# Layer 0 of a two-layer trunk: half of the gate projection z moved ahead of u, and all embedding units put into one block at the start

## Chip, core and metric

The kernel runs on one core of one Trainium2 chip. The metric is device time in microseconds (us), the median of the runs. Five engines matter: PE (TensorE, matmuls; PEld is its weight load), DVE (VectorE), ACT (ScalarE), POOL (GpSimd) and SP, which here only issues DMAs.

## What is computed

A trunk of two layers over two sequences of 512 tokens, model width 1024. The change lies in layer 0, a Fourier mixer with a gate, and in the embedding product that each layer adds at its end:

```
h = rmsnorm(x, norm_g[0])
u, z = split(h @ w_in)                       # 1024 channels each
f = real(fft2(u over tokens and channels in a group))   # 8 groups of 128
y = einsum('bsgc,gcd->bsgd', f, w_mix)
x = x + (y * silu(z)) @ w_out
x = x + sigmoid(x @ ple_gate_w[0]) * (p[0] @ ple_w[0])
```

Layer 1 (neighbourhood attention with the same kind of gate and embedding) and the final norm follow; the change does not touch them.

## The kernel before

Activations lie channel-major: 8 tiles of 128 channels by 1024 tokens, the two sequences s = 0 and 1 side by side, 512 tokens each. Every fp32 product is made of three passes (`PASSES`, line 29): each operand is split into a high part (a cast on ACT) and a low part (a subtraction on DVE or POOL; `split`, line 109), and high*high, high*low and low*high are accumulated. A product of one 128-channel output unit with one sequence over all 8 input tiles is thus 24 matmuls of 128x512.

**Embedding units.** `ple_units` (line 170) makes 16 units, n = 8*s + u, of 6 matmuls each: p[0] @ ple_w[0] for output tile u and sequence s. A unit is copied out of PSUM by ACT and stored to a DRAM scratch by SP. Before, three units come with the squares of x for the norm, and the others are handed out one at a time between the steps that follow (`next(ples)`).

**Norm.** The squares of x are made on ACT and added on DVE or POOL into accumulators (`sumsq`, line 160). `stats_sums` (line 139) adds them over channels with matmuls that have 2 columns; ACT takes the root, DVE the reciprocal (`stats_rows`), four PE transposes spread the row over partitions (`stats_bcast`) and ACT copies it to `rb`. This is done once for each sequence.

**Preparation of h.** For each item (k, s), tile k of sequence s: `h_scale` on DVE, `h_fold` (sums of token t and 512-t on DVE, differences on POOL, two single columns on POOL), `h_hi` (cast on ACT), `h_lo` (subtraction on DVE or POOL). The 16 items go in the order of `items` (line 257). h is kept folded, as even and odd parts over tokens.

**u.** Its weights are folded over channels in the same way (`w_fold`, line 282) and split (`w_split`, line 292). `u_step(hf, k)` (line 365) multiplies the folded h of tile k with half hf of the u weights: 27 matmuls of 252 or 260 columns into 7 PSUM banks. `first_half` (line 375) holds the order by hand: it interleaves the preparation of h, the folding of weights, the u steps of half 0 and the remaining embedding units. PE and DVE keep program order there (`pins`); ACT, POOL and SP are ordered by the compiler's scheduler. Half 1 follows, 8 more steps.

**Fourier products.** For each of 8 channel groups gi and each s: 12 matmuls into `z`, split, 6 matmuls into `yp`, and ACT copies `yp` to the tile y[gi] (line 481).

**z.** For u = 0 to 7 and each s, 24 matmuls into a PSUM tile `zg`, which uses h still in its folded form (line 497). Then the unfolding: ACT halves the odd part into `zo`, DVE makes three small operations into `zt`, ACT applies silu, DVE multiplies by y[u], and the result is split (cast on ACT, subtraction on POOL) into yz[u] (line 508). PE is not pinned there: the scheduler places z matmuls between Fourier products. The tiles of this stage (pools f2 and f2t) use memory that the Fourier stage holds to its end.

**Output.** For each of 8 output tiles and each s, 24 matmuls `og` over k = 0 to 7 of yz[k] (line 520). The weights of each z or output unit are loaded in two tiles of 256 KB, cast by ACT and split by POOL; four such tiles (`whl`) exist at a time.

Of the kernel before, what the change touches and what calls it, by code (L numbers as in the profile page):

```python
# [10 lines left out]
F32 = mybir.dt.float32  # L11
# [6 lines left out]
P = 128  # L18
# [14 lines left out]
def kernel(ctx: ExitStack, tc: tile.TileContext, xT, pT0, pT1, gains, w_u, w_l0, w_ple0,  # L33
# [35 lines left out]
    BM = ((KD - 1,), (0, KD - 1))  # L69
# [120 lines left out]
    # ------------------------------------------------------------------ layer 0: Fourier mixer  # L190
# [44 lines left out]
    ple_split(0)  # L235
    ples = ple_units(0, ph, plw, f0, ple_psum, PEB)
    for k in range(KD):
        sq = sumsq(accs[0], k, xk[k][:, 0:TOK], TOK, f0, v, hold=(k == 7), nb=SQB)
        if k in (3, 5, 7):
            next(ples)  # L240
    rw = stats_rows(stats_sums([accs[0], sq], TOK, f0, ups, "e10"), TOK, f0)
    next(ples)
    plw.append([])
    for raw in raws:
        hl = f0.tile([P, 2, 512], F32R, name="hl", tag="hlx", bufs=2)
        split(hl, raw, g)
        plw[1].append(hl)
    rbs = []

    def bcast(rw, tag):  # L250
        rb = f0.tile([P, TOK], F32, name="rb", tag="rb", bufs=2)
        a.copy(out=rb, in_=stats_bcast(rw, TOK, ups, tag))
        rbs.append(rb)

    bcast(rw, "e11")

    items = [(0, 0), (1, 0), (2, 0), (0, 1), (1, 1), (3, 0), (2, 1), (4, 0), (3, 1), (5, 0), (4, 1), (6, 0), (5, 1),
             (7, 0), (6, 1), (7, 1)]
# [22 lines left out]

    def w_fold(hf, k):
        raw = load_w(w_u[hf, k // 2, :, (k % 2) * 512:(k % 2 + 1) * 512])
        r4 = raw.rearrange("p (g c) -> p g c", g=4)
        wf = wfs[hf, k] = f1t.tile([P, 512], F32, name="wf", tag="wf", bufs=4)
        we = wf[:, 0:4 * NE].rearrange("p (g c) -> p g c", g=4)
        wo = wf[:, 4 * NE:].rearrange("p (g c) -> p g c", g=4)
        v.tensor_tensor(out=we[:, :, 1:64], in0=r4[:, :, 1:64], in1=r4[:, :, 127:64:-1], op=ALU.add)
        g.tensor_copy(out=we[:, :, 0:NE:64], in_=r4[:, :, 0:NE:64])
        g.tensor_tensor(out=wo, in0=r4[:, :, 1:64], in1=r4[:, :, 127:64:-1], op=ALU.subtract)  # L290
# [21 lines left out]
    accB = f0.tile([P, TOK], F32, name="accB")
    for k in range(KD):
        x = xk[k][:, TOK:TT]
        if k == 1:
            a.activation(out=accB, in_=x, func=AF.Square)
        elif k in (3, 5):
            sumsq(accB, k, x, TOK, f0, g, nb=SQB)
        else:
            sq = sumsq(accs[1], k, x, TOK, f0, v, hold=(k == 7), nb=SQB)  # L320
        for f in S1.get(k, ()):
            f()
    rw = stats_rows(stats_sums([accs[1], accB, sq], TOK, f0, ups, "o1"), TOK, f0)
# [51 lines left out]
    def first_half():  # L375
        kf, ks = iter(range(2, KD)), iter(range(2, KD))
        pins.update("pv")
        for i in range(3, len(items) + 2):
            if i - 1 < len(items) and i > 3:
                h_hi(*items[i - 1])  # L380
            if 5 <= i:
                h_lo(*items[i - 2], {'v': v, 'g': g}[LOE[i - 2]])
            if i < len(items):
                h_scale(*items[i])
                h_fold(*items[i])
            if i == 3:
                w_split(0, 1)
            if i in WFI:
                w_fold(0, next(kf))
            if i in WSI:  # L390
                w_split(0, next(ks))
            for k in range(KD):
                if (k, 0) in items[:max(0, i - 1)] and (k, 1) in items[:max(0, i - 1)] and k not in used and (0, k) in whs:
                    used.add(k)
                    next(ples, None)
                    u_step(0, k)
        for k in range(EW):
            w_fold(1, k)
            w_split(1, k)

    used = set()
    ych = []
    gps = Banks(z=(0, 1), yp=(2, 3), g=(4, 5, 6, 7), w=(4, 5, 6, 7, 0, 1, 2, 3))
    with c1:
        for hf in range(2):
            eps_[:] = [[ups_tile(f"e{s}{t}") for t in range(2)] for s in range(NSEQ)]
            ops_[:] = [ups_tile(f"o{s}") for s in range(NSEQ)]
            nps_[:] = [ups_tile("n")]
            if hf == 0:
                first_half()  # L410
            else:
                for k in range(KD):
                    if k >= EW:
                        w_fold(1, k)
                        w_split(1, k)
                    u_step(1, k)
                    if k == 1:
                        dc = load_tables(cs, sgn)
                    if k in (2, 5):
                        load_mix(k // 3, dc, qp)  # L420
            if hf == 0:
                for _ in ples:
                    pass
# [33 lines left out]
        for gi in range(8):  # L457
            y = xp.tile([P, TT], F32, name=f"y{gi}", tag=f"x{gi}")
# [3 lines left out]
            for s in range(NSEQ):  # L462
# [18 lines left out]
                a.copy(out=y[:, s * TOK:(s + 1) * TOK], in_=yp)  # L481
# [6 lines left out]
    with tc.tile_pool(name="f2", bufs=1) as f2, tc.tile_pool(name="f2t", bufs=2) as f2t:  # L488
        yz = []
        for u in range(8):  # L490
            hl = weights(w_l0[u])
            yzk = f2.tile([P, 2, TT], F32R, name=f"yz{u}")
            yz.append(yzk)
            for s in range(NSEQ):
                o = s * TOK
                ps = gps.tile([P, 512], F32, name="zg", tag="w")
                gemm(ps, hl, lambda k, al: h0[k][:, al, o:o + TOK])
                zo = f2t.tile([P, 256], F32, name="zo", tag="zo", bufs=1)
                a.activation(out=zo[:, 0:255], in_=ps[:, 257:512], func=AF.Copy, scale=0.5)
                z = f2t.tile([P, TOK], F32, name="zt", tag="zt")  # L500
                v.tensor_copy(out=z[:, 0:512:256], in_=ps[:, 0:512:256])
                v.scalar_tensor_tensor(out=z[:, 1:256], in0=ps[:, 1:256], scalar=0.5, in1=zo[:, 0:255],
                                       op0=ALU.mult, op1=ALU.add)
                v.scalar_tensor_tensor(out=z[:, 511:256:-1], in0=ps[:, 1:256], scalar=0.5, in1=zo[:, 0:255],
                                       op0=ALU.mult, op1=ALU.subtract)
                a.activation(out=z, in_=z, func=AF.Silu)
                v.tensor_tensor(out=z, in0=z, in1=ych[u][:, o:o + TOK], op=ALU.mult)
                split(yzk[:, :, o:o + TOK], z, g)
        for u in range(8):
            hl = weights(w_l0[8 + u])  # L510
# [51 lines left out]
    with tc.tile_pool(name="f3", bufs=1) as f3:  # L562
# [26 lines left out]
        block = gates(f3, 0, w_l0[16:24], x1h, emit0)  # L589
# [25 lines left out]
    # ------------------------------------------------------------------ layer 1: neighbourhood attention  # L615
# [18 lines left out]
    with ExitStack() as c2:  # L634
# [125 lines left out]
        # key tile, query blocks, and where in the step's pair of key tiles each query block lies  # L760
# [147 lines left out]
    # ------------------------------------------------------------------ layer 1: output, gate, final norm  # L908
# [211 lines left out]
def _layout(i):  # L1120
# [9 lines left out]
    w_l0 = np.concatenate([_units(w_in[:, 1024:]), _units(i["fn_w_out"][0]), _units(i["ple_gate_w"][0])], axis=0)  # L1130
# [7 lines left out]
    for sc in range(4):  # L1138
# [9 lines left out]
        "xT": c(xT), "pT0": c(pT0), "pT1": c(pT1), "gains": c(gains), "w_u": c(w_u), "w_l0": c(w_l0),  # L1148
# [26 lines left out]
```

## Time and profile before

| | before |
|---|---|
| median of 3 runs | 1128.08 us (1127.16 to 1130.82) |
| span of the profiled execution | 1125.8 us |
| PE busy | 1086.9 us, 97% |
| DVE, ACT, POOL busy | 568.8, 583.9, 629.3 us |
| mean granted clock of PE | 0.986 of full |

The profiled execution's own time is its span, 1125.8 us, plus what lies around it; the median of the runs is 2.3 us more than the span. Busy shares are averages over stages with different limits, so they say little about the first stage, which is the one that is edited. Idle time of an engine that does not bound a stage costs nothing.

### The profile page before, as it was taken

How to read it: one execution, taken by the hardware profiler on the slowest of the kernel's cores; microseconds unless marked ns; L12 is line 12 of the kernel's file. 1: busy time of each engine (PE TensorE's matmuls, PEld its weight loads, DVE VectorE, ACT ScalarE, POOL GpSimd, SP SyncE). 2: the span in 40 equal slices, each digit the busy share in tenths (PEclk: the TensorE clock that was granted, in tenths of full speed). 3: DMA queues.
4: the chain of work that ended last, by engine and by line, in shares of the span. 5: the costliest groups of instructions: out<-in, count | busy, mean ns of one | idle time of the engine just before them, and what ended most of it. 6: DMA issues, size and time to landing. Idle time of an engine off the chain costs nothing.

```text
span 1125.8 us, 17630 instructions
## 1 busy us (share of the span) xinstructions
PE 1086.9 (97%) x6028; PEld 934.5 (83%) x6028; DVE 568.8 (51%) x1253; ACT 583.9 (52%) x1083; POOL 629.3 (56%) x530
## 2 busy tenths in 40 slices
PE   6889999999999999999999999999999999999996
PEld 4779998888888888989888788989888886888886
DVE  5984015221123454277777666777766236114445
ACT  7434226332233474367777667768677734222434
POOL 4884216544534656455757475657566446548643
PEclk9889999999999999999999999999999998999998
DMA  8323002123244447547567565757674055322324
GB/s 318 106 89 109 29 20 75 56 60 109 85 146 144 158 151 224 150 128 198 172 170 214 153 197 163 199 167 209 172 217 123 21 196 197 126 97 78 103 65 150
DMA packets 75689, 156.04 MB, mean 139 GB/s; under 512 B 13328, under 2 KB 16016, under 8 KB 75600
## 3 DMA queue, kind: packets, MB, share of 16 engines
q1 hardware_dynamic: 64480, 128.43, 37.1%
q10 hardware_dynamic: 10960, 25.97, 8.0%
q8 instruction: 47, 0.77, 0.3%
q0 software_dynamic: 160, 0.52, 0.1%
q14 instruction: 42, 0.34, 0.1%
HBM read 107.17 MB, written 22.28 MB: 115 GB/s over the span
## 4 chain that ended last, share of the span: by engine, by line
PE 39%; DMA 6%; DVE 3%; ACT 2%; issue 1%; POOL 1%; SPq 0%; ACTq 0%; DVEq 0%; POOLq 0%
PE qg L82 8%; PE og L82 7%; PE gg L82 7%; PE vg L82 4%; PE ops L82 4%; PE zg L82 4%; PE pps L82 2%; PE sps L82 2%; DMA qst<-qh 2%; DMA qst<-ql 1%; DVE sz L82 1%; PE zs L82 1%; DVE x L82 1%; DMA raw<-in_w_na_dram 1%; DMA raw<-yz_d 1%
## 5 line engine op out<-in xcount | busy, mean ns | idle before, releaser
L82 POOL TENSOR_TENSOR hl<-raw,hl 128x512 fp32r<-128x512 f32 x168 | 223.2, 1332 | 181.8 <-ACT hl L82 163.8
L82 POOL TENSOR_TENSOR ptl<-st,pth 128x512 fp32r<-128x512 f32 x128 | 164.3, 1292 | 101.8 <-ACT pth L82 69.1
L82 PE MATMUL qg<-ha,hl 128*128 128x512 f32 x768 | 215.1, 396 | 0.0
L82 PE MATMUL gg<-ha,hl 128*128 128x512 f32 (+1 forms) x840 | 176.6, 371 | 0.0
L82 PEld LDWEIGHTS gg<-ha,hl 128*128 128x128 f32 x840 | 148.2, 188 | 27.2
L82 PE MATMUL zg<-ha,hl 128*128 128x512 f32 x672 | 164.8, 391 | 0.0
L82 ACT CAST hl<-raw 128x512 fp32r<-128x512 f32 x168 | 103.7, 618 | 112.8 <-PE og L82 34.5
L82 DVE CUSTOM_DVE_ANT_0 sps<-sps,bt 128x256 f32<-128x256 f32 x256 | 110.2, 430 | 72.9 <-PE sps L82 67.6
L82 PEld LDWEIGHTS qg<-ha,hl 128*128 128x128 f32 x768 | 130.3, 190 | 14.0
L82 PEld LDWEIGHTS zg<-ha,hl 128*128 128x128 f32 x672 | 121.6, 188 | 21.5
L82 PE MATMUL vg<-hl,ha 128*128 128x256 f32 x768 | 108.1, 282 | 0.0
L82 PEld LDWEIGHTS vg<-hl,ha 128*128 128x128 f32 x768 | 98.8, 190 | 0.1
L82 ACT ACTIVATE st<-st 128x512 f32<-128x512 f32 x128 | 80.8, 632 | 33.1 <-DVE st L82 32.0
L82 PE MATMUL og<-yzk,hl 128*128 128x512 f32 x384 | 91.1, 399 | 2.3 <-POOL yzk L82 1.2
L82 DVE TENSOR_TENSOR st<-pps,bt 128x512 f32<-128x512 f32 x128 | 87.0, 679 | 6.3 <-PE pps L82 6.2
L82 PEld LDWEIGHTS og<-yzk,hl 128*128 128x128 f32 x384 | 73.5, 193 | 19.7 <-POOL hl L82 1.9
L82 PE MATMUL og<-yz,hl 128*128 128x512 f32 x384 | 87.2, 389 | 0.0
L82 PEld LDWEIGHTS og<-yz,hl 128*128 128x128 f32 x384 | 72.1, 188 | 15.0
L82 ACT CAST pth<-st 128x512 fp32r<-128x512 f32 x128 | 79.5, 621 | 3.7 <-ACT qh L82 0.6
L82 DVE TENSOR_TENSOR sg<-sg,pg 128x512 f32<-128x512 f32 (+1 forms) x35 | 32.7, 934 | 87.1 <-ACT sg L82 87.1
L82 PE MATMUL ops<-ptl,vt 128*65 128x256 f32 x256 | 65.9, 280 | 0.0
L82 PE MATMUL ops<-pth,vt 128*65 128x256 f32 x256 | 65.9, 279 | 0.0
(154 smaller groups left out, 1688.4 us busy)
## 6 DMA issues: line engine op xcount, KB each, us to landing
bt<-in_bias_dram ACTq DMA_DIRECT2D x64, 384.0 KB
raw<-in_w_l_dram SPq DMA_DIRECT2D x80, 256.0 KB
raw<-in_w_na_dram SPq DMA_DIRECT2D x64, 256.0 KB
pp_d<-pe SPq DMA_DIRECT2D x32, 256.0 KB
pg<-pp_d SPq DMA_DIRECT2D x16, 512.0 KB
qst<-qh SPq DMA_DIRECT2D x64, 128.0 KB
kst<-kh SPq DMA_DIRECT2D x64, 128.0 KB
x<-in_xT_dram SPq DMA_DIRECT2D x16, 256.0 KB
```

Of the source, the lines that this page charges most:

```text
L82: ins = getattr(self.eng, op)(*args, **kw)
```

## The change

The embedding units become one block of 16 at the start. The table `beside` says what is issued behind each unit: squares, both norms, and the preparation of the first items of h. Outputs of units are copied in turn by DVE and ACT. The weights of the embedding are now all loaded ahead of x.

Then comes the preparation of the other items of h, and beside it z for u = 0 to 3 instead of u: `z_first(k, s)` makes 12 matmuls (4 units, 3 passes) for item (k, s), into 8 PSUM banks that hold the 4 units and both sequences. `z_out` copies them out (ACT), and `z_act` unfolds them and applies silu, beside the u steps of half 0. Half 0 of u now runs as half 1 does, after all of h is ready.

In the Fourier stage the first four groups are multiplied with silu(z) as they leave PSUM (DVE). In the z stage only u = 4 to 7 are left; each pass of its loop also splits y[u - 4]. The single-column copies in `h_fold` and `w_fold` go from POOL to ACT.

```diff
-    BM = ((KD - 1,), (0, KD - 1))
+    BM = ((0, KD - 1), (0, KD - 1))
-    pins.update(PINS)
-    plw = [weights(w_ple0[0])]
+    pins.update("pv")
+    raws = [load_w(w_ple0[0][:, 512 * i:512 * (i + 1)]) for i in range(2)]
     load_p(0)
+    for i in range(2):
+        raws.append(f0.tile([P, TOK], F32, name="h", tag="h", bufs=4))
+        sp.dma_start(out=raws[-1], in_=w_ple0[1][:, 512 * i:512 * (i + 1)])
     load_x(0)
-    raws = [load_w(w_ple0[1][:, 512 * i:512 * (i + 1)]) for i in range(2)]
+    load_p(1)
     load_x(1)
-    load_p(1)
...
+    def ple_out(n, pp, eng):
+        s, u = n // 8, n % 8
+        pe = f0.tile([P, TOK], F32, name="pe", tag="pe", bufs=PEB)
+        if eng is v:
+            v.tensor_copy(out=pe, in_=pp)
+        else:
+            a.copy(out=pe, in_=pp)
+        sp.dma_start(out=pp_d[0][u][:, s * TOK:(s + 1) * TOK], in_=pe)
...
-        g.tensor_copy(out=f[:, 0:512:256], in_=h[:, 0:512:256])
+        a.copy(out=f[:, 0:512:256], in_=h[:, 0:512:256])
...
+    def z_split(k, eng):
+        hl = whs["z", k] = whl.tile([P, 2, 512], F32R, name="hl", tag="hl")
+        split(hl, load_w(w_zk[k]), eng)
...
+    def z_first(k, s, us=range(4)):
+        o = s * TOK
+        for u in us:
+            if k == 0:
+                zps[u, s] = zbank.tile([P, 512], F32, name="zf", tag=f"z{u}{s}")
+            for n, (wl, al) in enumerate(PASSES):
+                mm(zps[u, s], whs["z", k][:, wl, u * P:(u + 1) * P], h0[k][:, al, o:o + TOK],
+                   start=(k == 0 and n == 0), stop=(k == KD - 1 and n == 2))
...
+    def z_out(u, s):
+        if s == 0:
+            zrs.append(xp.tile([P, TT], F32, name=f"zr{u}", tag=f"x{4 + u}"))
+        a.copy(out=zrs[u][:, s * TOK:(s + 1) * TOK], in_=zps.pop((u, s)))
+
+    def z_act(u, s):
...
+        v.tensor_tensor(out=z[:, 1:256], in0=r[:, 1:256], in1=r[:, 257:512], op=ALU.add)
+        g.tensor_tensor(out=z[:, 511:256:-1], in0=r[:, 1:256], in1=r[:, 257:512], op=ALU.subtract)
+        a.activation(out=z[:, 0:512:256], in_=r[:, 0:512:256], func=AF.Silu)
+        for c in (slice(1, 256), slice(257, 512)):
+            a.activation(out=z[:, c], in_=z[:, c], func=AF.Silu, scale=0.5)
...
+    def stat(s):
+        rws[s] = stats_rows(stats_sums([accs[s], accB, sqs[s]], TOK, f0, st_ps, "s"), TOK, f0)
...
+    beside = {
...
+        5: [L(ple_split, 1)],
+        6: [L(stat, 0), L(lambda: bcast(rws[0])), L(square, 0, 1), L(square, 1, 1)],
+        7: [L(h_scale, 0, 0), L(square, 2, 1)],
...
+        11: [L(h_hi, 1, 0), L(h_fold, 2, 0), L(square, 6, 1), L(square, 7, 1)],
+        12: [L(h_lo, 1, 0, g), L(h_hi, 2, 0)],
+        13: [L(stat, 1), L(z_split, 1, g)],
+        14: [L(lambda: bcast(rws[1])), L(h_lo, 2, 0, v)],
+        15: [L(h_scale, 0, 1), L(h_fold, 0, 1)],
+    }
+    prev = None
+    for n in range(16):
+        pp = ple0(n)
+        for f in beside[n]:
+            f()
+        if prev is not None:
+            ple_out(n - 1, prev, (a, v)[n % 2])
+        prev = pp
+    ple_out(15, prev, a)
...
+    for j, (k, s) in enumerate(steps0 + [(6, 1)]):
+        i = next(at)
+        if i < len(items):
+            if i > 3:
+                h_scale(*items[i])
+                h_fold(*items[i])
+            h_hi(*items[i])
+        if 4 <= i and i - 1 < len(items):
+            h_lo(*items[i - 1], (v, g)[i % 2])
+        if i in (4, 6, 8, 10, 12, 14):
+            z_split(i // 2, (g, v)[i // 2 % 2])
+        if k < 6 or s == 0:
+            z_first(k, s)
...
-            if hf == 0:
-                first_half()
...
+            for k in range(KD):
+                nk = k + EW
+                if nk < KD or hf == 0:
+                    w_fold(hf + nk // KD, nk % KD)
+                    w_split(hf + nk // KD, nk % KD)
+                u_step(hf, k)
+                if not hf:
+                    z_act(k // 2, k % 2)
...
-                a.copy(out=y[:, s * TOK:(s + 1) * TOK], in_=yp)
+                if gi < 4:
+                    v.tensor_tensor(out=y[:, s * TOK:(s + 1) * TOK], in0=yp, in1=y[:, s * TOK:(s + 1) * TOK], op=ALU.mult)
+                else:
+                    a.copy(out=y[:, s * TOK:(s + 1) * TOK], in_=yp)
...
-        for u in range(8):
-            hl = weights(w_l0[u])
+        for u in range(4, 8):
+            hl = weights(w_l0[u - 4])
...
-                split(yzk[:, :, o:o + TOK], z, g)
+                split(yz[u][:, :, o:o + TOK], z, g)
+                split(yz[u - 4][:, :, o:o + TOK], ych[u - 4][:, o:o + TOK], g)
```

## Rows read from the trace of the kernel before

**Rows 1.** Page, part 2, 40 slices: PE busy, and its granted clock, in tenths.

```profile
PE   6889999999999999999999999999999999999996
...
PEclk9889999999999999999999999999999998999998
```

**Rows 2.** Stretches: us, busy us (count) of PE, PEld, DVE, ACT, POOL; clock; DMA share; GB/s.

```profile
6.55:81.59 75.04, 63.73 (x361) 55.04 (x361) 61.04 (x80) 38.95 (x73) 56.67 (x70) 0.91 0.48 168
16.00:18.00 2.00, 2.00 (x17) 2.00 (x18) 0.00 (x0) 2.00 (x5) 1.82 (x2) 1.00 1.04 376
30.20:37.00 6.80, 5.27 (x15) 4.30 (x16) 6.12 (x7) 2.55 (x5) 6.63 (x8) 0.50 0.29 84
81.59:108.90 27.31, 27.31 (x222) 26.35 (x221) 14.21 (x27) 10.88 (x24) 13.40 (x19) 1.00 0.39 126
```

**Rows 3.** Waits of PE, first 110 us: us in total, times, longest.

```profile
PE u_e L82 <- DVE ha L82: 4.7, 3, 2.2
```

**Rows 4.** Timeline of PE: start us, us, line, operation, count, [idle before, releaser].

```profile
6.55 0.79 PE L82 MATMUL u_pp<-ph,hl 128*128 128x512 f32 x1 [6.55 <-ACT ph L82]
...
11.60 3.66 PE L82 MATMUL u_e<-ph,hl 128*128 128x512 f32 x12
...
26.72 1.05 PE L82 MATMUL st_ps<-ones,acc 128*128 128x2 f32 x8 [1.30 <-DVE acc L82]
...
28.53 1.03 PE L82 MATMUL st_ps<-ones,sq 128*128 128x2 f32 x8
...
31.73 1.11 PE L82 MATMUL rb<-ident,rs 128*128 128x128 f32 x4 [2.17 <-DVE rs L82]
...
32.50 2.91 PE L82 MATMUL u_pp<-ph,hl 128*128 128x512 f32 x6
...
42.02 1.55 PE L82 MATMUL u_pp<-ph,hl 128*128 128x512 f32 x6
...
43.41 0.40 PE L82 MATMUL u_e<-hl,ha 128*128 128x260 f32 x2
...
46.47 0.29 PE L82 MATMUL u_n<-hl,ha 128*65 128x260 f32 x1
...
169.74 61.16 PE L82 MATMUL zg<-ha,hl 128*128 128x512 f32 x269
```

**Rows 5.** DVE groups by form, 20.5 to 76 us: count, busy us, mean ns, idle before.

```profile
L82 DVE SCALAR_TENSOR_TENSOR h<-x,gain,rb 128x512 f32<-128x512 f32 x16 | 19.2, 1211 | 1.0 <-ACT rb L82 1.0
...
L82 DVE TENSOR_TENSOR f<-h 128x255 f32<-128x255 f32 x16 | 10.8, 679 | 0.4
...
L82 DVE TENSOR_TENSOR ha<-f,ha 128x512 fp32r<-128x512 f32 x8 | 7.0, 880 | 0.0
```

**Rows 6.** Timeline of DVE, two rounds of the first stage.

```profile
42.73 1.78 DVE L82 SCALAR_TENSOR_TENSOR h<-x,gain,rb 128x512 f32<-128x512 f32 x1
...
49.27 1.78 DVE L82 SCALAR_TENSOR_TENSOR h<-x,gain,rb 128x512 f32<-128x512 f32 x1
```

**Rows 7.** Timeline of the DMA queue of SP.

```profile
31.67 2.85 SPq L82 DMA_DIRECT2D raw<-in_w_u_dram  x2
```

**Rows 8.** Timeline of ACT, end of the Fourier products and after.

```profile
169.94 0.58 ACT L82 COPY y<-yp 128x512 f32<-128x512 f32 x1 [4.47 <-PE yp L82]
...
175.10 0.36 ACT L82 ACTIVATE zo<-zg 128x255 f32<-128x255 f32 x1
...
188.56 0.36 ACT L82 ACTIVATE zo<-zg 128x255 f32<-128x255 f32 x1
```

**Rows 9.** Timeline of DVE there: the product of z and y.

```profile
172.79 0.69 DVE L82 TENSOR_TENSOR zt<-zt,y 128x512 f32<-128x512 f32 x1 [1.13 <-ACT zt L82]
...
180.57 1.47 DVE L82 TENSOR_TENSOR zt<-zt,y 128x512 f32<-128x512 f32 x1 [0.76 <-ACT zt L82]
```

**Rows 10.** Timeline of POOL there.

```profile
174.28 1.29 POOL L82 TENSOR_TENSOR yz<-zt,yz 128x512 fp32r<-128x512 f32 x1 [11.44 <-ACT yz L82]
...
180.21 1.28 POOL L82 TENSOR_TENSOR yz<-zt,yz 128x512 fp32r<-128x512 f32 x1
```

More of the change, by code (lines that the diff above doesn't have):

```diff
@@ L32, with kernel @@
 @with_exitstack
-def kernel(ctx: ExitStack, tc: tile.TileContext, xT, pT0, pT1, gains, w_u, w_l0, w_ple0,
+def kernel(ctx: ExitStack, tc: tile.TileContext, xT, pT0, pT1, gains, w_u, w_zk, w_l0, w_ple0,
                       w_mix, dft_c, dft_s, w_na, w_z, bias, w_l1, w_ple1, out):
@@ L233, in ple_split, with ple0, bcast @@
             split2(ph[k][0][:, o:o + TOK], ph[k][1][:, o:o + TOK], pfs[k, s], v)
[L235 to L245, printed above, removed]
-        split(hl, raw, g)
-        plw[1].append(hl)
+    plw = [[], []]
+    for i, raw in enumerate(raws):
+        hl = whl.tile([P, 2, 512], F32R, name="hl", tag="hl")
+        split(hl, raw, g)
+        plw[i // 2].append(hl)
+        if i == 1:
+            ple_split(0)
+    ples_ps = Banks(p=(0, 1, 2, 3, 4, 5))
+    st_ps = Banks(s=(6,), r=(7,))
+    def ple0(n):
+        s, u = n // 8, n % 8
+        o, hl = s * TOK, plw[u // 4]
+        pp = ples_ps.tile([P, 512], F32, name="u_pp", tag="p")
+        ui = u % 4
+        gemm(pp, [hl[ui // 2][:, :, (ui % 2) * 256:(ui % 2 + 1) * 256]], lambda k, al: ph[k][al][:, o:o + TOK], ks=range(2))
+        return pp
+    def ple_out(n, pp, eng):
+        s, u = n // 8, n % 8
+        pe = f0.tile([P, TOK], F32, name="pe", tag="pe", bufs=PEB)
[4 more added lines that the diff above has]
+        sp.dma_start(out=pp_d[0][u][:, s * TOK:(s + 1) * TOK], in_=pe)
     rbs = []
-    def bcast(rw, tag):
+    def bcast(rw):
         rb = f0.tile([P, TOK], F32, name="rb", tag="rb", bufs=2)
-        a.copy(out=rb, in_=stats_bcast(rw, TOK, ups, tag))
+        a.copy(out=rb, in_=stats_bcast(rw, TOK, st_ps, "r"))
         rbs.append(rb)
-    bcast(rw, "e11")
-    items = [(0, 0), (1, 0), (2, 0), (0, 1), (1, 1), (3, 0), (2, 1), (4, 0), (3, 1), (5, 0), (4, 1), (6, 0), (5, 1),
-             (7, 0), (6, 1), (7, 1)]
     hs, fs, wfs, whs = {}, {}, {}, {}
@@ new lines, in z_unfold @@
+    def z_unfold(z, ps, pool):
+        zo = pool.tile([P, 256], F32, name="zo", tag="zo", bufs=1)
+        a.activation(out=zo[:, 0:255], in_=ps[:, 257:512], func=AF.Copy, scale=0.5)
+        v.tensor_copy(out=z[:, 0:512:256], in_=ps[:, 0:512:256])
+        v.scalar_tensor_tensor(out=z[:, 1:256], in0=ps[:, 1:256], scalar=0.5, in1=zo[:, 0:255],
+                               op0=ALU.mult, op1=ALU.add)
+        v.scalar_tensor_tensor(out=z[:, 511:256:-1], in0=ps[:, 1:256], scalar=0.5, in1=zo[:, 0:255],
+                               op0=ALU.mult, op1=ALU.subtract)
+        a.activation(out=z, in_=z, func=AF.Silu)
@@ L312, with square @@
     accB = f0.tile([P, TOK], F32, name="accB")
-    for k in range(KD):
-        x = xk[k][:, TOK:TT]
+    sqs, rws = {}, {}
+    def square(k, s):
+        x = xk[k][:, s * TOK:(s + 1) * TOK]
         if k == 1:
@@ new lines @@
+    at = iter(range(3, 24))
+    for j, (k, s) in enumerate(steps0 + [(6, 1)]):
[12 more added lines that the diff above has]
+        else:
+            for u in range(4):
+                z_first(6, 1, [u])
+                z_first(7, 1, [u])
+        if (k, s) in ((4, 1), (5, 1)):
+            w_fold(0, k - 4)
+        if (k, s) in ((5, 1), (7, 0)):
+            w_split(0, int(k == 7))
+        if (k, s) == (7, 0):
+            for u in range(4):
+                z_out(u, 0)
@@ L331, in load_tables @@
+    for u in range(4):
+        z_out(u, 1)
     def load_tables(cs, sgn):
@@ L373, in u_step @@
             u_bank(hl, k, *x)
[L375 to L401, printed above, removed]
     ych = []
@@ L408 @@
             nps_[:] = [ups_tile("n")]
-            if hf == 0:
-                first_half()
[L411 to L420, printed above, removed]
-            if hf == 0:
-                for _ in ples:
-                    pass
+            for k in range(KD):
[6 more added lines that the diff above has]
+                    z_act(k // 2, k % 2)
+                if hf and k == 1:
+                    dc = load_tables(cs, sgn)
+                if hf and k in (2, 5):
+                    load_mix(k // 3, dc, qp)
+            if hf == 0:
                 f0_ctx.close()
@@ L457 @@
         for gi in range(8):
-            y = xp.tile([P, TT], F32, name=f"y{gi}", tag=f"x{gi}")
+            y = zts[gi] if gi < 4 else xp.tile([P, TT], F32, name=f"y{gi}", tag=f"x{gi}")
             ych.append(y)
@@ L587, in finish0 @@
                 split(h1[k][:, :, o:o + TOK], h, g if k % 2 else v)
-        block = gates(f3, 0, w_l0[16:24], x1h, emit0)
+        block = gates(f3, 0, w_l0[12:20], x1h, emit0)
         pins.add("p")
```

61 lines of the change are left out of this document (25 added, 36 removed).

## Prediction

> **What bounds the kernel now.** I read the slices of the page first, then stretches of the start, PE's waits, its timeline, and last the helpers after the Fourier stage. PE is busy for nine tenths or more of nearly every slice from the fourth on; the granted clock dips in the second and third slice and hardly later [rows 1]. From PE's first matmul at 6.55 us to 81.59, where half 1 of u begins, 75.04 us pass and PE is busy 63.73 [rows 2]; in half 1 it is busy for every microsecond [rows 2]. What can be won lies before 81.59. It waits there 4.7 us for low parts of h from DVE, up to 2.2 at a time [rows 3]: DVE is busy 61.04 of the 75.04 us, POOL 56.67 [rows 2]. One round of that stage (two items of h, one weight tile) takes 49.27 - 42.73 = 6.54 us [rows 6], while PE has one u step and one unit for it: (46.47 - 43.41)/26 = 0.118 us a matmul, 27 are 3.18, plus 43.41 - 42.02 = 1.39 for a unit [rows 4], 4.6 in all. So the helpers set the pace, and the pauses cost clock on top: 30.2 to 37.0 ran at 0.50, 1.2 GHz for 2.4 [rows 2].
>
> **PE's slack before.** Necessary work in the 75.04 us: 16 units x 1.39 = 22.2; 8 steps x 3.18 = 25.4; five sums of squares at (28.53 - 26.72)/2 = 0.905 [rows 4], 4.5. Sum 52.1; slack 22.9 us (it includes the eight transposes, which stay).
>
> **z moved.** 192 matmuls at 61.16/269 = 0.227 us [rows 4] are 43.7 us, the same before u and behind it: nothing by themselves. What they buy is PE work beside the preparation of h, and u becomes as dense as half 1 is now.
>
> **The start, step by step (estimates from rows).** Unit 0 still waits for its inputs: 6.55 to 11.60, 3.7 over its 1.39. The next 12 matmuls take 3.66 against 2.78, 0.9 over [rows 4]. So unit 2 ends at 15.3, unit 6 at 20.8. Both norms are now written in PE's fixed order. For s = 0 the sums stand directly ahead of their transposes, with no unit between: 3 x 0.905 = 2.7, then root and reciprocal before PE can go on. Queued behind that wait are all other units and z. Before, the second norm paid 2.17 [rows 4], part of it because DVE was busy elsewhere. DVE now stands waiting for it; I take 1.0, bounds 0.5 and 2.2. Transposes: 32.50 - 31.73 = 0.77 at half clock [rows 4], so 0.4. Unit 7 starts at 24.9, unit 13 ends at 34.7. DVE starts the first h_scale at about 25.6 and has until then three scales (1.21), three folds (0.68), one low part (0.88) [rows 5], three adds (like the low part) and two unit copies (not shown; a product of that shape took 0.69 to 1.47 [rows 9], I take 0.69): 10.6 us, to 36.2. The last add gates the sums of s = 1, so PE waits 0 to 1.5; I take 0.7. The reciprocal of s = 1 is covered by unit 14. The block ends at 34.7 + 0.7 + 2.7 + 1.4 + 0.4 + 1.4 = 41.3.
>
> Slack after: 3.7 + 0.9 + 1.0 + 0.4 + 0.7 + 0.4 = 7.1. One more sum than before costs 0.9. Gain 22.9 - 7.1 - 0.9 = **14.9 us**, if the clock holds and z never waits.
>
> **Clock.** Sums of squares, whose matmuls have 2 columns, and waits did cost the clock: before the fall at 30.2 stood such sums and the 2.17 us wait [rows 2, 4]. With 1.8 us of sums the clock still stood at 1.00 [rows 2]. The new stretches are 2.7 + 1.0 + 0.4 and 0.7 + 2.7. I take a fall after each. Of the 6.8 us at half clock PE worked 4.5 (32.5 to 37.0), so lost 2.3. Two are 4.6; the first covers the 0.7 of PE's wait for DVE: 3.9. Bounds 0 and 2 x 3.4 = 6.8. Left: 11.0.
>
> **Does h keep up with z?** A pair of items is 24 matmuls, 5.4 us of PE. DVE per pair: two scales, two folds, one low part, half a z split: 2 x 1.21 + 2 x 0.68 + 1.5 x 0.88 = 5.1 [rows 5], without the weight folding that filled part of the 6.54. POOL also loses the single-column copies. The tight place is item (0, 1), third in z: wanted at 41.3 + 5.4 = 46.7, and ready at about 45.2 (`rb` at 40.5, two scales, two folds, a low part). I take no wait; if a pair went on taking 6.54, each item would lose (6.54 - 5.45)/2 = 0.55, the last one, 12 items on, 6.6 less the lead of 1.5 and the 0.7 by which (6, 1) goes first: 4.4 us late (below). ACT gains the small copies, eight PSUM copies and three silu calls for each z_act; it was busy 38.95 of 75 [rows 2], so nothing. z_act lies beside half 0 of u, where half 1 shows DVE at 14.2 and POOL at 13.4 of 27.3 [rows 2].
>
> **Loads and queues.** The half megabyte of embedding weights ahead of x delays it by 0.52 MB / 376 GB/s = 1.4 us [rows 2]; the sums are not reached before 20.8, so units cover it. The eight loads of z weights move from a quiet stretch into 20 to 60 us. On SP a load that waits for its buffer holds the unit stores behind it, and those hold the seven output buffers (`PEB`); before, one pair of such loads took 2.85 us on the queue [rows 7]. Seven units are 9.7 us of PE, so it is covered: price 0, at most 2.85. On POOL, no DMA is moved.
>
> **The price: the end of z.** The unfolding can't begin before the Fourier stage ends; POOL waited 11.44 us there and its first yz comes at 174.28, with 269 z matmuls still to run from 169.74 [rows 4, 10]. Before, 61 us of z covered that backlog. Of the 384, 115 were placed between Fourier products, four tiles and part of a fifth, which took the banks that were free; the same 115 of now 192 leave 77, 17.5 us, and eight tiles and 16 splits must pass in them, eight of these splits new. Tile after tile started (188.56 - 175.10)/5 = 2.69 us apart [rows 8], and one took 180.21 + 1.28 - 175.10 = 6.4 from its first operation to its split [rows 8, 10]. Counted from 169.74: tile 7 (u = 7, s = 0) starts near 0.7 + 6 x 2.69 = 16.8 and is split at 23.2; the first output product wants it after 17.5 + 21 x 0.227 = 22.3: 0.9 late. POOL must do 14 splits and two weight tiles by then, 16 x 1.29 = 20.6 [rows 10]. It starts between 0.7 (the y tiles 0 to 3 are ready) and 4.5 (as before); I take 3.3, nearer to the row: 23.9. If yz[3] is last, PE stops at 17.5 + 2.0 = 19.5 and waits 4.4; if POOL takes the ready y tiles first, 1.6. I take **3.0**, bounds 0 and the second rival's 6.3.
>
> **Sum.** 14.9 - 3.9 - 3.0 = 8.0 us of 1125.8: span 1117.8, and with 2.3 around it 1120.1. Later stages see the same order and move up unchanged.
>
> **Rivals.**
> 1. *h still sets the pace, and PE's waits only move from u to z.* For it: DVE at 5.1 of 5.4 us, and an order written out by hand. Against: the folding is gone from the round. At 6.54 a pair PE loses 4.4: 1120.1 + 4.4 = 1124.5. Chance 0.14.
> 2. *POOL blocks DVE after the Fourier stage.* The product of z and y took 0.69 alone and 1.47 beside a POOL split [rows 9, 10]. With POOL never idle each tile would pay a whole split: 2.69 less a mean product of 1.08 is 1.61, plus 0.69 + 1.29 = 3.59 a tile; tile 7 is split at 0.7 + 21.5 + 6.4 = 28.6, 6.3 late: 1128.1 - 11.0 + 6.3 = 1123.4. Chance 0.14. The Trainium skill (SBUF — State Buffer, Who interferes with whom) has it as a rule: a DVE instruction with two SBUF inputs and a GpSimd instruction that reads SBUF exclude each other for the whole of one. By that rule the sum would be this rival's; the two products above agree; the distance of 2.69 is a mean over tiles of both kinds.
> 3. *Slower: the extra split joins each tile's chain.* If the scheduler queues the cast (a copy of that shape took 0.58 [rows 8]) and the subtraction (1.29) of y[u - 4] between one tile and the next, tiles start 2.69 + 1.87 = 4.6 apart; yz[3] follows at 0.7 + 27.6 + 6.4 + 1.3 = 36.0, 16.5 after PE stops for it at 19.5: 11.0 - 16.5 = -5.5, 1133.6. It decides from a distance of about 3.7 us on. For it: ACT and POOL aren't pinned, and program order is just this. Against: these splits are ready early and fill gaps. Chance 0.12.
> 4. *No fall of the clock, nothing lost after Fourier*: 1128.1 - 14.9 = 1113.2. Chance 0.10.
>
> **How the numbers follow.** The forecast has 0.50, from 1115 to 1124 by the bounds of its terms; of the like cases I count the share that crosses 0.3% (3.4 us, about what a measurement can tell from no change). Faster: 0.48 of the forecast, 0.10 of rival 4, half of rivals 1 and 2, together 0.72, less 0.02 for what I haven't seen. Slower: 0.12 and 0.01. Same: 0.17. The range 1112 to 1131 leaves out rival 3 and little else.
>
> **What would show it.** Right: units end near 41 to 46 us; PE hardly waits for h between there and 90; half 0 of u is as dense as half 1; one or two dips of the clock near 23 to 45; PE waits 2 to 5 us for yz at the first output products. Wrong: waits of z_first for h tiles add up to more than 3 us (rival 1); products of z and y near 2 us (rival 2); tiles 4 us apart (rival 3); or the block of units ends after 50.

## The result and the profile after

The changed kernel takes 1117.15 us (median of 4 runs, 1113.6 to 1121.33); the kernel before, run beside it, 1129.45. The ratio is 0.9893, with a 95% interval of 0.9858 to 0.9927. The profiled execution spans 1112.9 us, 12.9 less than before. Where that comes from is read off the first matmul of each stage (PE's timeline of both kernels):

| PE begins | before | changed | earlier by |
|---|---|---|---|
| output products of layer 0 | 230.74 | 219.22 | 11.52 |
| gates of layer 0 | 317.77 | 306.26 | 11.51 |
| q products of layer 1 | 429.44 | 417.93 | 11.51 |
| z products behind the attention | 896.93 | 886.45 | 10.48 |
| end of the span | 1125.8 | 1112.9 | 12.9 |

So 11.5 us are won before the output products and kept to 0.01 us up to layer 1. In layer 1 PE's order is the one of before; what it adds or takes (1.0 us lost, 2.4 won) is treated with the runs below.

Page of the changed kernel, part 2, 40 slices, to be held against [rows 1]:

```profile
PE   7999999999999999999999998999999999999996
...
PEclk9999999999999999999999999999999999999998
```

The second and third slices are full now, and the dip of the clock is gone at this scale. PE's timeline at the start, to be held against [rows 4]:

```profile
7.49 1.95 PE L82 MATMUL u_pp<-ph,hl 128*128 128x512 f32 x3 [7.49 <-ACT ph L82]
9.71 11.41 PE L82 MATMUL u_pp<-ph,hl 128*128 128x512 f32 x39 [0.28 <-ACT ph L82]
20.96 0.95 PE L82 MATMUL st_ps<-ones,acc 128*128 128x2 f32 x8
...
24.27 1.12 PE L82 MATMUL rb<-ident,rs 128*128 128x128 f32 x4 [0.57 <-DVE rs L82]
25.03 11.17 PE L82 MATMUL u_pp<-ph,hl 128*128 128x512 f32 x42
36.64 1.02 PE L82 MATMUL st_ps<-ones,acc 128*128 128x2 f32 x8 [0.44 <-DVE acc L82]
...
42.64 0.85 PE L82 MATMUL zf<-ha,hl 128*128 128x512 f32 x3
43.93 43.13 PE L82 MATMUL zf<-ha,hl 128*128 128x512 f32 x189 [0.43 <-DVE pe L82]
86.90 0.87 PE L82 MATMUL u_e<-hl,ha 128*128 128x260 f32 x6
```

Seven units, sums, transposes, seven units, sums, two units, and then 192 matmuls of z with one wait of 0.43 us: PE never waits for h, where [rows 3] had 4.7. Units 7 to 13 take 11.17 us where 42 matmuls at the pace of z (43.13/189 = 0.228) need 9.6; the granted clock says why, for most of it. Stretches of 1 us of the changed kernel (columns as in [rows 2]):

```profile
24.00:25.00 1.00, 0.73 (x4) 0.74 (x5) 0.18 (x1) 0.67 (x2) 0.81 (x1) 0.59 1.02 387
25.00:26.00 1.00, 1.00 (x4) 0.84 (x3) 0.00 (x0) 1.00 (x2) 0.45 (x1) 0.50 1.07 395
26.00:27.00 1.00, 1.00 (x4) 0.77 (x3) 0.96 (x1) 0.00 (x1) 0.82 (x1) 0.50 1.00 380
27.00:28.00 1.00, 1.00 (x5) 0.82 (x4) 1.00 (x3) 0.59 (x2) 0.55 (x1) 0.71 0.32 117
```

About 3 us at 1.2 GHz behind the first norm, and no second fall. PE at the junction of z and u, then at the end of z:

```profile
88.30 1.25 PE L82 MATMUL u_e<-hl,ha 128*128 128x260 f32 x6
89.80 0.95 PE L82 MATMUL u_o<-hl,ha 128*128 128x252 f32 x6 [0.26 <-ACT zr L82]
...
113.63 2.89 PE L82 MATMUL u_e<-hl,ha 128*128 128x260 f32 x23
...
201.75 17.64 PE L82 MATMUL zg<-ha,hl 128*128 128x512 f32 x77
219.22 87.20 PE L82 MATMUL og<-yz,hl 128*128 128x512 f32 x384
```

Exactly 77 z matmuls are left behind the Fourier products, as the prediction had counted, and the 384 output matmuls (16 products of 24) follow in one stretch of 87.20 us without a gap. POOL there, to be held against [rows 10]:

```profile
202.57 10.98 POOL L82 TENSOR_TENSOR yz<-zt,yz 128x512 fp32r<-128x512 f32 x8 [7.72 <-ACT yz L82]
...
214.76 1.29 POOL L82 TENSOR_TENSOR yz<-zt,yz 128x512 fp32r<-128x512 f32 x1
...
231.28 1.30 POOL L82 TENSOR_TENSOR yz<-zt,yz 128x512 fp32r<-128x512 f32 x1
...
233.87 1.29 POOL L82 TENSOR_TENSOR yz<-zt,yz 128x512 fp32r<-128x512 f32 x1 [1.28 <-ACT yz L82]
```

POOL first splits all eight ready y tiles in one go and only then serves the unfolding; on DVE's side that is this wait ahead of the third tile:

```profile
216.08 0.16 DVE L82 COPY zt<-zg 128x2 f32<-128x2 f32 x1 [4.93 <-POOL yz L82]
```

The last split ends at 235.16, 16 us after the output products began. Yet PE has no gap. How that can be is the subject of the experiments on the order of the output products.

### The profile page after: what moved, and what is told of

It is laid out like the page before. It is cut to its first block, busy times and chain, and to the rows that moved or that the text cites. A ratio compares the mean times of both kernels' runs of the same rounds, so it can differ in the third digit from the quotient of the medians.

```text
span 1112.9 us, 17647 instructions
## 1 busy us (share of the span) xinstructions
PE 1081.7 (97%) x6036; PEld 930.2 (84%) x6036; DVE 572.3 (51%) x1246; ACT 581.5 (52%) x1115; POOL 621.3 (56%) x504
## 4 chain that ended last, share of the span: by engine, by line
PE 40%; DMA 5%; DVE 3%; ACT 2%; issue 1%; SPq 0%; POOL 0%; ACTq 0%; DVEq 0%; POOLq 0%
PE qg L82 9%; PE og L82 7%; PE gg L82 7%; PE ops L82 4%; PE zg L82 4%; PE vg L82 4%; PE pps L82 2%; PE sps L82 2%; DMA qst<-ql 2%; DVE sz L82 1%; PE zs L82 1%; DVE x L82 1%; DMA raw<-in_w_na_dram 1%; DMA raw<-yz_d 1%; DVE st L82 1%
## 5 line engine op out<-in xcount | busy, mean ns | idle before, releaser
L82 POOL TENSOR_TENSOR hl<-raw,hl 128x512 fp32r<-128x512 f32 x163 | 218.2, 1343 | 151.1 <-ACT hl L82 144.6
L82 PE MATMUL zg<-ha,hl 128*128 128x512 f32 x480 | 121.3, 392 | 0.0
L82 PEld LDWEIGHTS zg<-ha,hl 128*128 128x128 f32 x480 | 85.6, 188 | 14.0
L82 PE MATMUL og<-yzk,hl 128*128 128x512 f32 x384 | 88.4, 390 | 2.6 <-POOL hl L82 1.4
L82 PEld LDWEIGHTS og<-yzk,hl 128*128 128x128 f32 x384 | 71.7, 188 | 19.1 <-POOL hl L82 2.3
L82 PEld LDWEIGHTS og<-yz,hl 128*128 128x128 f32 x384 | 72.1, 188 | 14.9
L82 PE MATMUL pps<-qst,kst 98*128 98x256 f32 x256 | 57.6, 307 | 8.9 <-DVE st L82 7.5
```

The costliest lines, as they stand in the source:

```text
L82: ins = getattr(self.eng, op)(*args, **kw)
```

## Experiments

All positions are read from PE's timeline; up to the q products of layer 1 they repeat between runs except for the clock and the first loads. Two runs are the changed kernel itself. Runs are named by the first part of their label, as e5. The edits e3, e4, e7, e9 and e11 were run once each, for their traces; their single times (1122.94, 1121.11, 1116.83, 1126.27 and 1119.41 us) decide nothing.

**The changed kernel again (a0, a1).**

> The changed kernel once more, on the chip of the experiments, so that they can be compared with it under the same conditions. Expected: 0.989 of the kernel before, about 12 us less; one fall of the clock near 24 us; the output products begin at about 219 us without a wait.

> The changed kernel once more, beside the next one. Both theories: 1113 to 1123 us, median about 1116; z begins 34.3 to 36.4 us behind the first matmul, by whether the granted clock falls behind one norm or behind both.

a0 takes 1115.01 us (4 runs, ratio 0.9856, 0.9813 to 0.9898) and a1 1117.4 us (6 runs, 0.9867, 0.9825 to 0.9908). z begins 35.5 and 34.2 us behind the first matmul (the second is 0.1 below what was expected); the output products begin at 218.95 and 218.07. Each shows one fall of the clock in the first 100 us, behind the first norm. The q products of layer 1 begin at 417.65 and 416.77, but the attention up to the z products behind it takes 470.14 in one and 464.63 in the other (468.52 above). Of the 5.6 us between the spans of these two profiled runs (1114.4 and 1108.8), 5.5 lie in that stage.

**The block of units alone (e5).** z stays behind the Fourier products, half 0 of u stands beside the preparation again, without units in it:

```
-    for j, (k, s) in enumerate(steps0 + [(6, 1)]):
...
-            z_first(k, s)
+    def first_half():
...
+                    u_step(0, k)
```

> One part of the change alone: the block of 16 units with its table, loads, norms and the small copies on ACT stays; z for all eight u is behind the Fourier stage again, and u half 0 lies beside the preparation of h, as in the kernel before but without units to fill its waits. Theory A (z is what fills PE while h is prepared): the block ends at about 42.6 us as in the changed kernel, then 6.5 rounds of 5.5 to 6.5 us and the last steps follow, half 1 of u begins at 82 to 90 us against 81.6 before and an equal of 70.1 in the changed kernel; 0 to 8 us slower than the kernel before, 12 to 20 slower than the changed one. Theory B (the dense block of units, not z, brings the gain): half 1 begins near 72, and the time is about that of the changed kernel.

1136.67 us, ratio 1.0043 (1.0016 to 1.007): slightly slower than before, and 21.7 above a0, a little more than the 12 to 20 of theory A. PE's waits of the first 100 us, and two of its stretches:

```profile
PE u_e L82 <- ACT ha L82: 7.3, 4, 2.5
PE u_e L82 <- DVE ha L82: 4.5, 5, 1.7
```

```profile
60.00:70.00 10.00, 6.39 (x36) 5.80 (x36) 9.90 (x13) 4.42 (x11) 6.66 (x8) 0.83 0.16 53
70.00:80.00 10.00, 6.46 (x40) 6.05 (x40) 9.90 (x12) 3.27 (x9) 7.15 (x7) 0.85 0.17 52
```

Half 1 of u begins at 87.83, before at 81.59. With the units gone from between the u steps PE is busy 6.4 of 10 us, waits 11.8 us for h, and the clock falls. So the block alone wins nothing; the gain needs z as PE's work beside the preparation. Whether z would win as much without the block is not shown: no run has it so.

**Is h close to being late again (e4, e11)?** Two edits. In e4 the copies of single columns in the folds go back to POOL, in `h_fold` (2 columns) and likewise in `w_fold` (8):

```
-        a.copy(out=f[:, 0:512:256], in_=h[:, 0:512:256])
+        g.tensor_copy(out=f[:, 0:512:256], in_=h[:, 0:512:256])
```

> The changed kernel with the copies of 2 and of 8 columns in the folds given back to POOL (0.40 us each there, 0.20 on ACT). Theory A (the preparation of h runs at the pace of z with almost no margin: its last part is written at 81.03 us and first used at about 81.3 us): TensorE waits for ha in the last third of the z stretch, 1 to 4 us in all, and half 0 of u begins that much later than 86.62 us. Theory B (POOL, which sits idle 10.5 us behind DVE's h in this stretch, takes the copies for nothing): no wait for ha, half 0 of u begins at 86.4 to 86.8 us.

and in e11 all low parts of h in the z stretch go to DVE:

```
-            h_lo(*items[i - 1], (v, g)[i % 2])
+            h_lo(*items[i - 1], v)
```

> The changed kernel with all the low halves of h on DVE in the z stretch: six operations of about 1.0 us leave POOL for DVE, about 6 us. Theory A (DVE, busy 9.5 to 9.9 of 10 us there, sets the pace of h, with about 1.2 us of margin at the end): TensorE waits 3 to 5.5 us for ha, and half 0 of u begins 47.2 to 49.8 us behind the first z product instead of 44.25. Theory B (the round through DVE, POOL and ACT sets it, and DVE merely runs slowly because it shares with POOL): relieving POOL pays for it, 0 to 1 us of wait.

With the copies on POOL, z begins at 40.60 and half 0 of u at 85.02: 44.4 us, against 44.25 in a0, and no wait for h (the copies took 430 ns each, 5.6 us in all). That is theory B's result, but not for nothing: the margin is used up. In a0 the last low part ends at 81.03 and the first z matmul that reads it (the 173rd of 192) begins at 82.09; in e4 these are 80.30 and 80.35. The junction of z and u got longer too, by this wait of PE for ACT's copies of z:

```profile
88.03 0.63 PE L82 MATMUL u_e<-hl,ha 128*128 128x260 f32 x3 [0.80 <-ACT zr L82]
```

so that the Fourier products begin 99.46 us behind z, in a0 98.26. With all low parts on DVE, 44.06 us and again no wait, and the last low part is ready 2.1 us ahead of its first use: the 3 to 5.5 us of wait that theory A asked for did not come, although DVE is busy 9.8 to 9.9 of 10 us up to 72 us. DVE's groups from 42 to 87 us tell why; first the changed kernel (a0), then with the six operations moved:

```profile
L82 DVE SCALAR_TENSOR_TENSOR h<-x,gain,rb 128x512 f32<-128x512 f32 x13 | 15.7, 1206 | 0.9 <-ACT rb L82 0.9
L82 DVE TENSOR_TENSOR f<-h 128x255 f32<-128x255 f32 x13 | 8.4, 649 | 0.4
L82 DVE TENSOR_TENSOR ha<-f,ha 128x512 fp32r<-128x512 f32 x7 | 7.2, 1029 | 0.6 <-ACT ha L82 0.6
```

```profile
L82 DVE TENSOR_TENSOR ha<-f,ha 128x512 fp32r<-128x512 f32 x13 | 14.8, 1139 | 0.0
L82 DVE SCALAR_TENSOR_TENSOR h<-x,gain,rb 128x512 f32<-128x512 f32 x13 | 10.7, 821 | 2.3 <-ACT rb L82 2.3
L82 DVE TENSOR_TENSOR f<-h 128x255 f32<-128x255 f32 x13 | 5.5, 425 | 0.4
```

Six more low parts cost DVE 7.6 us, and the other two groups gave back 7.9: h fell from 1206 to 821 ns, f from 649 to 425. So part of DVE's busy time came with POOL's work beside it: the same operation on the same shape is shorter when POOL has less to do. The Trainium skill (SBUF — State Buffer, Who interferes with whom) has a rule for this: a DVE instruction with two SBUF inputs contends with a GpSimd instruction that reads SBUF; the trace agrees in direction, and the price here is about 0.4 us per h.

**Order of the output products (e1).** In the changed kernel the scheduler doesn't run one output product after another. DVE's adds, which take each finished product out of PSUM, show it; two lines of before, then of the changed kernel:

```profile
236.38 0.69 DVE L82 TENSOR_TENSOR x<-og,xr 128x512 f32<-128x512 f32 x1 [2.52 <-PE og L82]
241.82 0.69 DVE L82 TENSOR_TENSOR x<-og,xr 128x512 f32<-128x512 f32 x1 [4.75 <-PE og L82]
```

```profile
235.29 1.29 DVE L82 TENSOR_TENSOR x<-og,xr 128x512 f32<-128x512 f32 x2 [2.15 <-PE og L82]
237.56 0.69 DVE L82 TENSOR_TENSOR x<-og,xr 128x512 f32<-128x512 f32 x1 [0.98 <-PE og L82]
241.18 0.69 DVE L82 TENSOR_TENSOR x<-og,xr 128x512 f32<-128x512 f32 x1 [2.94 <-PE og L82]
```

Before, the first add comes 5.6 us behind the first output matmul and the next 5.44 later, the time of 24 matmuls: one product after the other. In the changed kernel the first comes 16.1 us behind, and four products end by 241.18, when 96 matmuls are done (219.22 + 96 x 0.227 = 241.0): the first four were open in PSUM together until the late tiles were there. The experiment holds PE to the written order:

```
+        pins.add("p")
         for u in range(8):
...
+        pins.discard("p")
```

> The changed kernel with one edit: the matmuls of the output stage keep the order in which they are written (product after product, k from 0 to 7). Theory A (the unfolding of z really ends late, and only the freedom to begin several output products hides it): in the changed kernel the first product would reach k = 6 at about 223.8 us, where yz[6] is split at 227.1, and then yz[7] at 232.6. So PE waits some 8 us in two or three waits for yz, and the time rises by 6 to 9 us over the changed kernel. Theory B (the splits come in time anyway): no wait over 1 us, no change of time.

1129.82 us, ratio 0.9971 (0.9944 to 0.9998). PE's timeline:

```profile
218.96 4.24 PE L82 MATMUL og<-yz,hl 128*128 128x512 f32 x18
225.42 0.49 PE L82 MATMUL og<-yz,hl 128*128 128x512 f32 x1 [2.23 <-ACT yz L82]
226.77 0.73 PE L82 MATMUL og<-yz,hl 128*128 128x512 f32 x2 [0.86 <-POOL yz L82]
230.51 0.80 PE L82 MATMUL og<-yz,hl 128*128 128x512 f32 x1 [3.00 <-ACT yz L82]
231.86 83.99 PE L82 MATMUL og<-yz,hl 128*128 128x512 f32 x362 [0.55 <-POOL yz L82]
315.68 14.67 PE L82 MATMUL gg<-ha,hl 128*128 128x512 f32 x64
```

From the first output product to the gates it is 96.72 us instead of 87.04: 6.64 of waits and 3 of clock (0.50 from 229 to 235). The free order is worth 9.7 us here, most of what the change gains. The median is 14.8 above that of the changed kernel in the same series. Where the other 5 lie is not shown for the median; in the two profiled runs, 19.1 apart, the rest lies in the attention, 479.79 us against 470.14, with PE's order in it unchanged. Against the shortest attention (a1, 464.63) PE waited there 15.2 us instead of 7.4, most of it for DVE's `st`, and the clock stood at 0.50 for 10 us in two falls where a1 has none. Why these differ is open.

**Who makes the tiles late (e9, e3)?** The same order, with the splits of the eight y tiles on DVE (e9):

```
-                split(yz[u - 4][:, :, o:o + TOK], ych[u - 4][:, o:o + TOK], g)
+                split(yz[u - 4][:, :, o:o + TOK], ych[u - 4][:, o:o + TOK], v)
```

> Output matmuls pinned to the written order as in e1_og_order, and the eight y tiles of the first four z units split by DVE instead of POOL. In e1_og_order the output stage waits 6.6 us in four places and the gates begin at 315.68 us instead of 305.99 us. Theory A (those waits exist because POOL takes the eight ready y tiles, 11 us of work, ahead of the unfolding): the last unfolding split ends about 8 to 10 us earlier, the output matmuls wait at most 1 us, the gates begin at 306.0 to 307.0 us. Theory B (the unfolding's own chain over ACT, DVE and POOL is the slow part, about 2.4 us per tile and more when DVE takes the y tiles): waits of 3 us or more stay and the gates begin at 309 us or later.

```profile
218.34 4.92 PE L82 MATMUL og<-yz,hl 128*128 128x512 f32 x21
226.12 0.79 PE L82 MATMUL og<-yz,hl 128*128 128x512 f32 x1 [2.86 <-ACT yz L82]
227.47 84.61 PE L82 MATMUL og<-yz,hl 128*128 128x512 f32 x362 [0.56 <-POOL yz L82]
311.92 18.30 PE L82 MATMUL gg<-ha,hl 128*128 128x512 f32 x80
```

The stage takes 93.58 us; 3.1 of the 9.7 come back. The last split ends at 229.98 instead of 234.37, 4.4 earlier, not 8 to 10. Theory B has the larger part: the unfolding's own distance stays (2.6 us a tile, (228.70 - 210.35)/7) and makes tile 7 late, and POOL's splits ahead of it add to that. What this run doesn't take apart is ACT, whose casts of the y tiles still stand ahead of the unfolding (six of them 3.22 us, up to the first silu). The same edit with the order left free (e3):

> The changed kernel with the eight y tiles of the first four z units split by DVE instead of POOL, output order free. Theory A (behind the Fourier part nothing but TensorE bounds the changed kernel, because the free order of the output products already covers the late tiles): the gates begin at 305.7 to 306.3 us as in the changed kernel (305.99), although the last unfolding split ends 8 to 10 us earlier. Theory B (the late tiles still cost something, for example through the interleaved products): the gates begin 1 to 3 us earlier.

The gates begin at 305.91 (305.99 in a0) from output products that begin at 218.87 (218.95): theory A. The last split ends at 230.94 instead of 234.86, 3.9 earlier and not 8 to 10, and these 3.9 are worth nothing.

**The clock at the norms (e7, e2).** In e7 the three sums stay together, and only the transposes of the first norm are put behind one more unit:

```
-        6: [L(stat, 0), L(lambda: bcast(rws[0])), L(square, 0, 1), L(square, 1, 1)],
+        6: [L(stat, 0), L(square, 0, 1), L(square, 1, 1)],
+        7: [L(lambda: bcast(rws[0])), L(h_scale, 0, 0), L(square, 2, 1)],
```

> The changed kernel with only the four transposes of the first norm moved behind one more embedding unit; the three sums stay together (24 products of 2 columns, 2.6 us). Theory A (the one fall of the granted clock, 24.2 to 27.4 us, follows the sums, the wait for the root and the transposes taken together, 4.1 us; the second norm, whose sums are followed by a unit, shows none): no fall; z begins about 2.0 us earlier than the changed kernel's 42.37 us (1.5 of clock and 0.6 of wait), that is at 40.2 to 40.6 us. Theory B (the sums alone are enough): the fall stays, z begins 0.4 to 0.8 us earlier.

The fall stays, it even comes earlier, and there is a second one:

```profile
21.72 2.91 PE L82 MATMUL u_pp<-ph,hl 128*128 128x512 f32 x6
...
38.35 2.62 PE L82 MATMUL u_pp<-ph,hl 128*128 128x512 f32 x6
...
43.24 0.87 PE L82 MATMUL zf<-ha,hl 128*128 128x512 f32 x3
```

A unit takes 1.4 us at full clock. z begins 36.3 us behind the first matmul, no earlier than in the changed kernel. Theory B: in this run the fall came behind 2.7 us of products with 2 columns with no wait after them. They don't always bring it: in e9 the same sums, with a wait of 0.57 behind them, were followed by none in the first norm. Next, in e2, the same sums spread, each behind a unit of its own (both norms):

```
-    def stat(s):
...
+        sps[s] = st_ps.tile([P, 512], F32, name="st_ps", tag="s")
...
+        4: [L(square, 6, 0), L(square, 7, 0), L(part, 0, 0)], 5: [L(part, 0, 1), L(ple_split, 1)],
+        6: [L(part, 0, 2), L(root, 0), L(square, 0, 1), L(square, 1, 1), L(square, 2, 1)],
```

> The changed kernel with the three sums of each norm put behind three units (accB, acc, last square) instead of one after the other, the transposes of s = 0 one unit later, and the squares of s = 1 one unit earlier. Theory A (the stretch of 24 narrow matmuls plus the wait for the root makes the clock fall at 24 us): no fall before 60 us, the wait of 0.6 us for the root is gone, z begins 1.5 to 2.5 us earlier than in the changed kernel, and the time falls by as much. Theory B (the fall has another cause): the clock falls at about the same time, and with rb one unit later nothing is won, or up to 1 us lost.

```profile
19.16 0.95 PE L82 MATMUL st_ps<-ones,acc 128*128 128x2 f32 x8
19.97 1.63 PE L82 MATMUL u_pp<-ph,hl 128*128 128x512 f32 x6
21.44 0.95 PE L82 MATMUL st_ps<-ones,sq 128*128 128x2 f32 x8
22.24 1.63 PE L82 MATMUL u_pp<-ph,hl 128*128 128x512 f32 x6
...
38.92 0.85 PE L82 MATMUL zf<-ha,hl 128*128 128x512 f32 x3
```

No fall in the first 46 us, no wait for the root; z begins 3.45 us earlier than in the changed kernel beside it, more than expected, and the output products 3.11 (215.84). The median, 1115.24 us (0.9841, 0.9808 to 0.9873), does not show it: a0 has 1115.01.

**A version to beat both (e12)**: the spread sums, the copies of z's second half from PSUM by ACT and DVE in turn (against the wait at 89.80), and the first weights loaded just ahead of the p tiles that meet them.

> Three edits on the changed kernel: the sums of each norm behind three units (as in e2_spread), the copies of the second half's z from PSUM alternately on ACT and DVE, and the first weights and the first p tiles loaded in the order in which the first units use them. Theory A (what is left at the head is worth its sum, because TensorE waits for nothing else up to the attention): 3.1 us from the sums, 0.3 to 0.7 from the copies, 0.4 to 0.8 from the loads; the q products of layer 1 begin at 413.0 to 413.9 us instead of 417.65, and the median lies 3 to 5 us below that of the changed kernel. Theory B (the attention, whose length varies by several us between runs with the same order, takes the gain back): the q products begin as early, but the median is within 1 us of the changed kernel.

1113.11 us (6 runs, 1110.05 to 1118.79; ratio 0.9843, 0.9803 to 0.9884), 4.3 below the changed kernel beside it, though the intervals of the two ratios overlap. The q products begin at 413.92, 2.85 earlier than there: theory A at its lower end. The loads won nothing that shows (first matmul at 6.94, in e2 at 6.93); the copies moved the wait (0.39 at `u_n`) and brought the Fourier products to 98.12 us behind z, in e2 98.60. Over all series the two versions with spread sums have a mean of 1114.1 us in 12 runs, the changed kernel 1116.8 in 14: 2.7 apart, with a 95% interval of about 2.5 to either side, which fits the 2.85 and 3.11 of the positions.

## Why the prediction was right, step by step

1120.1 us were forecast, 1117.15 came, inside the range and on the side that had 0.70; the gain is 12.3 us in the medians where 8.0 were forecast. The forecast's mechanism held: z as cover for the preparation of h. Its terms:

- **PE's slack.** Unit 6 ends at 20.96, predicted 20.8; the first sums take 2.74 up to the wait, predicted 2.7; the waits were 0.57 and 0.44, I had taken 1.0 and 0.7; without falls of the clock the block was to end at 41.3; it ended at 42.64 with one. Right.
- **Not priced**: 0.43 us where z meets the bank that DVE's copy of a unit has to free; at the junction of z and u 0.26 of wait and 1.25 - 0.87 = 0.38 of a stretched group, because ACT must empty z's banks; and half 0 of u, from 86.90 to 113.63 less that 0.64, takes 26.1 us, 0.7 more than 8 x 3.18. Together 1.8.
- **Clock, 3.9.** One fall in this run: 1.1 us in units 7 to 13 (11.17, where e9 kept the full clock and took 10.05) and 0.4 in the transposes ahead of them (0.76 from their start to the unit, in e9 0.40), 1.5 in all. The step was right that the sums endanger the clock, and oversized for this run: how many falls there are varies. Nine profiled runs have PE's order of this block; five had one fall behind the first norm (after, a0, a1, e1, e4), e9 one behind the second, and e3, e5 and e11 both, as the prediction had taken it; in e5 and e11 the first was about twice as long.
- **h keeps pace: 0.** Right; rival 1 is excluded by the waits, and the two edits leave it without a wait even with more work on POOL or on DVE. But it holds by about 1 us (1.06 between the last low part and its use in a0, 0.05 in e4). The reason I gave was only half of it: the 5.1 of 5.4 us were taken from rows in which DVE ran beside POOL, and e11 shows the same operations shorter.
- **Loads and queues: 0.** Right, as far as the waits show.
- **The end of z, 3.0: the step that failed, twice.** The sign that I had named for it, waits of 2 to 5 us for yz at the first output products, did not come. The count of 77 matmuls and the distance of 2.69 were right: the unfolding's splits come (233.87 - 214.76)/7 = 2.73 us apart. But POOL took all eight y tiles first, 11 us, so yz[7] for s = 0 was split 30.8 us after 201.75, not 23.9: DVE waited 4.93 us for POOL ahead of the third tile, and the 23.9 had POOL's splits follow one another at 1.29 without waiting for tiles 2.7 apart. In the written order that costs 9.7 us, 6.64 of it waits, as e1 shows; for just this order of POOL I had worked out 1.6. And I took the written order for granted, since the trace of before shows it there. The scheduler owns PE's order in that stage and opened other products instead: measured price 0. That was luck and not foresight: in the order that I took for granted the change would have gained next to nothing (e1, ratio 0.9971).
- **Sum.** 14.9 less 1.3 (block later, mostly clock), 1.8 and nothing at the end of z is 11.8; measured 11.5. The forecast's 8.0 differ by the 3.0 of the failed step and by a clock term that was too large by 2.4 in this run, against 1.8 that I had not seen.
- **Rivals.** 2: the product of z and y takes 0.73 to 1.48 us in the changed kernel, 1.43 or more in four of eight, so the mechanism is there, but the distance stayed 2.73, not 3.59, and PE had other work. 3: the extra splits did not fall between the tiles; they came ahead of all of them, and the mechanism of a late yz was real in the written order, where it would have taken the gain: 1129.82 against 1131.63 before. 4: nothing was lost after Fourier, as it said, but one fall was left; its 1113.2 are the nearest of the rivals, a little farther off than the forecast.

The last 1.4 us of the 12.9 in the two profiled runs are not shown to be the change's: with PE's order unchanged in both, the attention took 464.6 to 479.8 us over thirteen profiled runs, and what follows it 226.4 to 228.9. PE's waits and the falls of the clock there differ between runs; what makes them differ is open.

## What to carry to other kernels

Where helpers set the pace of a stage, look for independent work of the bounding engine that needs only what is ready there, and move it beside them: the gain is the slack of that stage, less what the new junctions cost. Before pricing a late operand, ask who owns the order: with independent products and free PSUM banks a scheduler hides in one stage what a fixed order pays in full (9.7 us here). Try matmuls of few columns spread between full ones instead of together: here it brought the output products 3.1 us forward.

## What the runs showed of the hardware

- Twenty-four matmuls of 2 columns in a row, 2.7 us, without a gap, were followed by about 3 us at 1.2 GHz (e7, 0.50 from 22 to 25 us); the same 24 with six full matmuls behind each eight kept 2.4 GHz (e2 and e12, both norms), where the ten profiled runs with the sums together had 14 falls at 20 norms. Whether a fall comes is not a property of the program alone: with the same order at the start there were one or two, in different places. For the rise at the start of a kernel, the Trainium skill (TensorE: Matmul & The Clock Gate, Part 1) says that the point of the transition shifts from run to run because the chip's observation does not start with the kernel; the runs show such a shift: their matmuls go from 0.43 us each to 0.23 at 3.7 us (e9) to 6.9 us (a0) behind the first one. That the falls vary for the same reason, no run here shows.
- A busy share of DVE near 99% did not mean that nothing more fitted: with six more operations on DVE and six fewer on POOL, the three groups above took 31.0 us instead of 31.3.
- A stage in which PE's order is fixed and which ran without change (the attention) varied by 15 us, more than the whole gain; some 8 of these were PE's waits (7.4 us in a1, 15.2 in e1), up to 5 the clock. For changes of this size the positions ahead of such a stage say more than single times.
